# A convolution mixer's input projection computed two output blocks at a time in seven block products

## The chip, the cores and the metric

The kernel runs on one core of a Trainium2 chip. The metric is device time in microseconds of one execution; the kernel before took 1708.74 us, the median of three runs (1708.41 to 1710.8).

## The reference

Two request groups, 512 and 256 tokens, pass through a two-layer encoder trunk with model width 1024, as one row of 768 tokens. Layer 0 mixes tokens by windowed attention, layer 1 by a gated convolution of width 3. Each layer goes on with a squared-ReLU MLP of width 4096 and a gated per-layer embedding added to the residual. The change lies in the convolution mixer:

```python
def rms_norm(x, g):
    y = xf * lax.rsqrt(jnp.mean(xf * xf, axis=-1, keepdims=True) + EPS)
    return (y * g.astype(jnp.float32)).astype(x.dtype)

def short_conv(h, w_in, conv_w, w_out):
    b_gate, c_gate, u = jnp.split(h @ w_in, 3, axis=-1)
    z = c_gate * u
    zp = jnp.pad(z, ((0, 0), (half, half), (0, 0)))
    conv = zp[:, 0:s] * conv_w[0]
    for t in range(1, CONV_WIDTH):
        conv = conv + zp[:, t:t + s] * conv_w[t]
    return (b_gate * conv) @ w_out

x = x + short_conv(rms_norm(x, norm_mix[1]), conv_w_in[0], conv_w[0], conv_w_out[0])
```

`w_in` is 1024 x 3072. The convolution runs over each request group by itself.

## The kernel before

The activations lie transposed: 8 blocks of 128 channels (partitions) by 768 tokens, the residual `x(m)` in SBUF throughout. Every matrix product is computed in float32 from two-part operands: `hi` is the value rounded by ScalarE (ACT) to the matmul's `fp32r` type, `lo` is the rest, a subtraction on VectorE (DVE), and a product is `hi*hi + hi*lo + lo*hi`, three matmuls on TensorE (PE), accumulated in PSUM (`split`, `group2`). One matmul takes 128 x 128 weights and 384 tokens, half of the 768 (`H`).

The stages stand one after the other: attention, MLP 0, the gated embedding of layer 0 (`ple`), the convolution mixer (`mixer_conv`), MLP 1, the last gated embedding. Weights come from HBM in pieces of 128 x 1024 (512 KB) through three buffers (`wraw`, line 89, on SyncE's queue), and are split into `whi`/`wlo`.

In `ple`, each of 8 blocks is a gate product of 48 matmuls. Then DVE multiplies with the inverse root `rstd` (L1198), ACT takes the sigmoid (L1199), DVE multiplies with the projected embedding `pr` (L1200) and adds to `x` (L1202). `Norm.block` writes the scaled block as `hi` and `lo` (`xs_mix`, L186, L187) for the convolution, and adds its squares to an accumulator (`acc_mix`, L196). The root of the sum of squares comes later: `acc_parts` splits the accumulator (`ah`, `al`), PE sums over partitions with a matrix of ones (`ss`, L235), and DVE and ACT make `rstd` (L252 to L267). Until then products go on without it; it is multiplied into their results.

`mixer_conv` goes through 8 blocks `m`. Each takes three groups of 48 matmuls (L129): `c` with weight block 8 + m, `u` with 16 + m, `b` with m. DVE multiplies `c` with the squared `rstd` (L1281), with `u` into `z` (L1290, a row of 771 with zero columns between the groups), takes three taps of `z` (L1293 to L1295), scales `b` (L1300), multiplies both (L1301, L1302) and the result is split (`ys`, L83 and L84). Then `project_add` makes the 8 blocks of `w_out` from them, adds them to `x` (L813), and makes MLP 1's normed input.

The two MLPs already use a seven-product scheme for a product of 2 x 2 blocks of matrices (a variant of Strassen's). `Weights7` fetches two weight pieces, forms four weight sums on DVE (L392 to L398) and splits weights and sums in the groups `direct`, `second`, `s32`, `s14`, `w22`. `Norm7` keeps the normed input as four quarters (`x11`, `x12`, `x21`, `x22`) and four combinations of them (`t1` to `t4`, one `combine` per pair of blocks). `product7` (L449) is one of the seven products, 12 matmuls; PSUM banks `a`, `b`, `c`, `d` carry them, and ACT copies one bank to another (L1046, L1053, L1058) where two results share a part. The first two jobs of an MLP (`up_plain`, L978) are plain products of 96 matmuls, since combinations and `rstd` aren't there yet.

What sets the order: in the MLPs the order on PE, DVE and ACT is that of the code (`manual_schedule`); in `ple`, `mixer_conv` and `project_add` a scheduler places the instructions. SyncE's queue is always placed by it.

Of the kernel before, what the change touches and what calls it, by code (L numbers as in the profile page):

```python
# [11 lines left out]
F32 = mybir.dt.float32  # L12
F32R = mybir.dt.float32r
AF = mybir.ActivationFunctionType
ALU = mybir.AluOpType
# [32 lines left out]
def trunk_kernel(ctx: ExitStack, tc: tile.TileContext, a: dict, out: bass.AP):  # L48
# [792 lines left out]
    def first_chunk(l, norm, early):  # L841


        w = []

        def behind(i):
            if i == 4:
                w.append(up_chunk(l, 0))
# [61 lines left out]

    def mlp(l, norm, nxt, w, places, early, product=None):
# [43 lines left out]
        def up_plain(u, w, make, then):  # L955
# [11 lines left out]

            order = [(i, ks, (0, 1)) for i in range(2) for ks in ((0, 6), (6, 8))]
            if known or parts:
                order = [(i, (0, 8), (o,)) for i in range(2) for o in (1, 0)]  # L970
            for n, (i, ks, sides) in enumerate(order):
                for k in range(*ks):
                    m, h = PAIRED[k] % (KB // 2), PAIRED[k] // (KB // 2)
                    c = slice(P * m, P * m + P)
                    hi, lo = w.w[f"w{i + 1}{h + 1}"]
                    for j, (wt, part) in enumerate(((hi, 0), (hi, 1), (lo, 0))):
                        for o in sides:
                            pe.matmul(  # L978
                                ps[i][o],
                                lhsT=wt[:, c],  # L980
                                rhs=xs[f"x{h + 1}{1 + o}"][m][part],
                                start=k == 0 and j == 0,
                                stop=k == KB - 1 and j == 2,
                            )
# [45 lines left out]

        def up(u, w, make, then):


            first = u == PLAIN[l]
            w.low("s32")
            w.split("s14")
            if not first:
                late()
            v = make()
            seven = isinstance(v, Weights7)  # L1040
            a = bank("A", "a")[:, :H]
            product7(a, w, "w11", xs, True)
            if not first:
                late()
            c = bank("A" if first else "C", "c")[:, :H]
            act.activation(c, a, AF.Copy)  # L1046
            late(3 if first else 1)
            w.split("w22")
            late()
            b = bank("A" if first else "B", "b")[:, :H]  # L1050
            product7(b, w, "s3", xs, True)
            p = big("p")[:, :H]
            act.activation(p, b, AF.Copy)  # L1053
            if seven:
                v.sums32()
            product7(a, w, "s2", xs, False)
            d = bank("B", "d")[:, :H]
            act.activation(d, a, AF.Copy)  # L1058
            late(2)
            if seven:  # L1060
                v.sums14()
                v.high("s32")
            late()
            product7(c, w, "w12", xs, False)
            if seven:
                v.high("direct")
            product7(a, w, "s1", xs, False)
            y1, y2 = big("y1"), big("y2")
            dve.tensor_tensor(y2[:, H:], a, p, ALU.add)  # L1069
            rectified(y1, c, 0, H, ALU.max)  # L1070
            late()
            if seven:
                v.low("direct")
            else:
                v = [then(0)]
            product7(d, w, "w22", xs, False)
            dve.tensor_tensor(y2[:, :H], d, p, ALU.add)
            rectified(y2, y2[:], 0, T, ALU.min)
            squared(y2)
            product7(a, w, "s4", xs, False)  # L1080
            rectified(y1, a, H, T, ALU.max)
            pend.extend(acts_of(u, y1, y2, y1))
            return v
# [182 lines left out]
    def mixer_conv(norm, nxt, places, held, behind):  # L1266
        ys = [], []
        r = None
        Z = T + 3
        for m in range(KB):  # L1270
            cp = both("c")
            group2(cp, terms_of(weight(a["w_in"][KB + m], KB), norm.xs))
            up = both("u")
            group2(up, terms_of(weight(a["w_in"][2 * KB + m], KB), norm.xs))
            if r is None:
                r = norm.rstd(psum)
                r2 = slot(held[4], "rstd2", F32)
                act.activation(r2[:], r, AF.Square)
            c = big("c")
            for t, o, e in pieces(cp):  # L1280
                dve.tensor_tensor(c[:, o:e], t, r2[:, o:e], ALU.mult)  # L1281
            z = slot(held[m % 2], "z", F32, Z)
            y = slot(held[2 + m % 2], "y", F32, Z)
            s0, s1 = SEQS
            for o in (0, s0 + 1, T + 2):
                nc.gpsimd.memset(z[:, o : o + 1], 0.0)

            for o, e in ((0, H), (H, s0), (s0, T)):
                k, i = 1 + (o >= s0), o // H
                dve.tensor_tensor(z[:, o + k : e + k], c[:, o:e], up[i][:, o - i * H : e - i * H], ALU.mult)  # L1290

            n = T + 1
            dve.tensor_scalar(y[:, :n], z[:, 0:n], tap(0, m), None, ALU.mult)  # L1293
            dve.scalar_tensor_tensor(y[:, :n], z[:, 1 : 1 + n], tap(1, m), y[:, :n], ALU.mult, ALU.add)
            dve.scalar_tensor_tensor(y[:, :n], z[:, 2 : 2 + n], tap(2, m), y[:, :n], ALU.mult, ALU.add)  # L1295
            bp = both("b")
            group2(bp, terms_of(weight(a["w_in"][m], KB), norm.xs))
            b = big("b")
            for t, o, e in pieces(bp):
                dve.tensor_tensor(b[:, o:e], t, r[:, o:e], ALU.mult)  # L1300
            dve.tensor_tensor(b[:, :s0], b[:, :s0], y[:, :s0], ALU.mult)  # L1301
            dve.tensor_tensor(b[:, s0:], b[:, s0:], y[:, s0 + 1 : n], ALU.mult)  # L1302
            hi, lo = (slot(places[8 * p + m], "ys") for p in range(2))
            split(hi[:], lo[:], b[:])
            ys[0].append(hi[:])
            ys[1].append(lo[:])
        project_add(a["w_out"], ys, nxt, behind)
# [128 lines left out]
```

## Time and profile before

| | |
|---|---|
| median of the runs | 1708.74 us (1708.41 to 1710.8) |
| the profiled execution | 1711.21 us |
| its span, first to last instruction | 1709.4 us |
| mean granted TensorE clock | 0.994 |
| HBM read | 123.10 MB |

A row of the profile names the line of the kernel, the engine, the operation and its operands by the program's names, with buffer numbers left out. PEld is the loading of weights into TensorE. "Busy" is the time in which an instruction of the engine ran; matmuls overlap one another, so PE's pace is read from starts, not from lengths. In a row of a timeline the first number is the start, the second the length of the row (of several instructions, where it ends in x2 or more), and what stands in brackets is the idle time before it and what ended it. A row of the waits gives the total, the number and the longest.

### The profile page before, as it was taken

What the parts mean: (1) busy time and instruction counts of PE and PEld (TensorE: products, weight loads), DVE (VectorE), ACT (ScalarE), POOL (GpSimd) and SP (SyncE); (2) the same over time, 40 slices, a digit from 0 to 9 for tenths busy, and PEclk for the clock granted to TensorE, in tenths of its full rate; (3) what the DMA queues carried; (4) which work ended last, traced back from release to release, by engine and by line L of the source; (5) the groups of instructions that cost most, each with busy time, mean ns of one, the idle gap of its engine ahead of it and who ended that gap; (6) DMA issues with size and microseconds to landing.
All of it is one profiled execution on the core that took longest, in us unless ns stands there. A gap on an engine that the chain in (4) does not pass through costs nothing.

```text
span 1709.4 us, 24198 instructions
## 1 busy us (share of the span) xinstructions
PE 1670.7 (98%) x9542; PEld 1614.4 (94%) x9542; DVE 1346.6 (79%) x2207; ACT 858.9 (50%) x1370; POOL 2.0 (0%) x30
## 2 busy tenths in 40 slices
PE   8999999989999999999999999999999999999996
PEld 7887788989999999999999999999999999999986
DVE  6588888899999999977764444658989999999676
ACT  6367756755555445445541111445455555545454
POOL 0000000000000000000000000000000000000000
PEclk9999999999999999999999999999999999999998
DMA  8654322211222122122311111211221222212222
GB/s 259 192 138 121 115 68 81 87 54 70 74 75 73 64 74 75 66 85 88 108 62 62 62 65 67 79 50 50 74 74 64 73 75 74 70 67 87 75 89 96
DMA packets 47842, 144.59 MB, mean 85 GB/s; under 512 B 6080, under 2 KB 10688, under 8 KB 47728
## 3 DMA queue, kind: packets, MB, share of 16 engines
q1 hardware_dynamic: 45168, 139.89, 24.8%
q10 hardware_dynamic: 2560, 3.15, 0.7%
q8 instruction: 75, 1.23, 0.3%
q14 instruction: 39, 0.32, 0.1%
HBM read 123.10 MB, written 10.48 MB: 78 GB/s over the span
## 4 chain that ended last, share of the span: by engine, by line
PE 66%; DVE 23%; ACT 7%; issue 2%; DMA 0%; SPq 0%; DVEq 0%; ACTq 0%
PE a L449 14%; PE mm L129 9%; PE mm L138 8%; PE gate L129 4%; PE b L129 4%; PE c L129 4%; PE u L129 4%; PE C L449 3%; PE B L449 3%; PE b L449 3%; DVE t L344 3%; DVE wlo L428 3%; DVE y L921 3%; PE gate L138 3%; DVE zlo L428 2%
## 5 line engine op out<-in xcount | busy, mean ns | idle before, releaser
L83 ACT ACTIVATE whi<-wraw 128x1024 fp32r<-128x1024 f32 (+2 forms) x73 | 75.5, 1034 | 185.2 <-PE b L129 53.0
L417 ACT ACTIVATE whi<-sum 128x1024 fp32r<-128x1024 f32 x56 | 59.0, 1053 | 146.6 <-PE a L449 146.6
L924 ACT ACTIVATE y<-y 128x768 f32<-128x768 f32 x64 | 53.6, 838 | 139.8 <-DVE y L921 139.8
L449 PE MATMUL a<-act,whi 128*128 128x384 f32 x448 | 96.7, 337 | 0.0
L449 PE MATMUL a<-t,zhi 128*128 128x384 f32 x448 | 92.4, 338 | 3.7 <-ACT c L1046 3.7
L449 PE MATMUL b<-t,zhi 128*128 128x384 f32 x448 | 92.2, 337 | 2.6 <-ACT zhi L417 2.6
L84 DVE TENSOR_TENSOR wlo<-wraw,whi 128x1024 fp32r<-128x1024 f32 (+2 forms) x73 | 87.0, 1192 | 9.5 <-ACT whi L83 9.1
L449 PE MATMUL a<-t,whi 128*128 128x384 f32 x448 | 91.9, 337 | 0.0
L449 PE MATMUL a<-xs,whi 128*128 128x384 f32 x448 | 87.6, 337 | 0.8 <-DVE y L1069 0.8
L1102 DVE TENSOR_TENSOR x<-x,a 128x384 f32<-128x384 f32 x112 | 60.8, 553 | 33.8 <-PE a L449 33.5
L449 PEld LDWEIGHTS a<-t,zhi 128*128 128x128 f32 x448 | 79.2, 188 | 4.3 <-ACT c L1046 4.3
L138 PE MATMUL mm<-xs_mix,whi 128*128 128x512 f32 (+1 forms) x320 | 82.9, 342 | 0.0
L449 PEld LDWEIGHTS b<-t,zhi 128*128 128x128 f32 x448 | 79.4, 188 | 2.9 <-ACT zhi L417 2.9
L449 PEld LDWEIGHTS a<-xs,whi 128*128 128x128 f32 x448 | 79.0, 188 | 1.2 <-DVE y L1069 1.2
L449 PEld LDWEIGHTS a<-act,whi 128*128 128x128 f32 x448 | 79.8, 188 | 0.0
L449 PEld LDWEIGHTS a<-t,whi 128*128 128x128 f32 x448 | 79.0, 188 | 0.0
L428 DVE TENSOR_TENSOR wlo<-wraw,whi 128x1024 fp32r<-128x1024 f32 x60 | 73.2, 1220 | 5.3 <-ACT whi L417 5.3
L428 DVE TENSOR_TENSOR wlo<-sum,whi 128x1024 fp32r<-128x1024 f32 x56 | 68.4, 1222 | 9.4 <-ACT whi L417 9.4
L338 ACT ACTIVATE t<-y 128x768 fp32r<-128x768 f32 x56 | 47.1, 842 | 46.1 <-DVE y L329 35.7
L417 ACT ACTIVATE whi<-wraw 128x1024 fp32r<-128x1024 f32 x60 | 63.2, 1053 | 12.1 <-PE C L449 6.5
L428 DVE TENSOR_TENSOR zlo<-sum,zhi 128x1024 fp32r<-128x1024 f32 x56 | 68.2, 1217 | 0.0
L417 ACT ACTIVATE zhi<-sum 128x1024 fp32r<-128x1024 f32 x56 | 59.3, 1059 | 16.5 <-DVE sum L393 16.5
(290 smaller groups left out, 4629.2 us busy)
## 6 DMA issues: line engine op xcount, KB each, us to landing
wraw<-in_up SPq DMA_DIRECT2D x64, 512.0 KB, 3.5
wraw<-in_down SPq DMA_DIRECT2D x64, 512.0 KB, 3.5
wraw<-in_w_in SPq DMA_DIRECT2D x24, 512.0 KB, 3.5
wraw<-in_gate SPq DMA_DIRECT2D x16, 512.0 KB, 3.5
pj<-pjs SPq DMA_DIRECT2D x16, 384.0 KB, 3.1
wraw<-in_w_q SPq DMA_DIRECT2D x8, 512.0 KB, 5.0
wraw<-in_w_out SPq DMA_DIRECT2D x8, 512.0 KB, 3.5
x_in<-in_x SPq DMA_DIRECT2D x8, 384.0 KB, 7.0
```

Source lines behind the costliest of these rows:

```text
L83: first = act.activation(hi, src, AF.Copy)
L84: dve.tensor_tensor(lo, src, hi.bitcast(F32), ALU.subtract)
L129: pe.matmul(t, lhsT=w, rhs=x[:, o:e], start=first and i == 0 and j == 0, stop=last and i == n - 1 and j == 2)
L138: pe.matmul(ps[:, o:e], lhsT=w, rhs=x[:, o:e], start=i == 0 and j == 0, stop=i == n - 1 and j == 2,)
L338: act.activation(t[0][:], (self.q1, self.q2)[i][:], AF.Copy)
L344: dve.tensor_tensor(lo[:], (self.q1, self.q2)[i][:], hi[:].bitcast(F32), ALU.subtract)
L417: act.activation(hi[:], src, AF.Copy)
L428: dve.tensor_tensor(lo[:], src, hi[:].bitcast(F32), ALU.subtract)
L449: pe.matmul(ps, lhsT=a, rhs=b, start=start and i == 0, stop=i == len(terms) - 1, skip_group_check=True)
L921: dve.scalar_tensor_tensor(t[:, o:e], src, 0.0, r[:, o:e], op, ALU.mult)
L924: act.activation(t[:], t[:], AF.Square)
L1102: dve.tensor_tensor(t[:, o : o + H], t[:, o : o + H], f, op)
```

## The change

The projection's blocks are taken two at a time: weight blocks `m` and `m + 1` of `c`, of `u` and of `b` are one job each (`conv_chunk`), 12 jobs in all. The first two (`c` and `u` of blocks 0, 1) are plain products of 96 matmuls, the other ten take the seven products of 12. `up`'s body becomes `seven_parts`, shared by both, with the handling of results in a class (`Squares` in the MLP, `Out` here); `up_plain`'s loop becomes `plain_order` and `plain_product`. The convolution's normed input `n3` is now a `Norm7`: quarters, and combinations 0 (made during `ple`), 1, 2, 3 (made during the two plain jobs). `ple` goes through the blocks in the order 0, 4, 1, 5, 2, 6, 3, 7, and fetches and splits the first job's weights. The order on PE, DVE and ACT in `mixer_conv` is now that of the code. The first tap runs on ACT. The products `b * conv` are kept in float32 (`ys`) and split only during the last job and after it (`whole`), in places that products have freed by then.

```diff
-    def project_add(w, src, norm, behind):
+    def project_add(w, first, src, norm, behind):
         for i, m in enumerate(PAIRED):
             ps = both()
-            group2(ps, terms_of(weight(w[m], KB), src))
+            group2(ps, terms_of(weight(w[m], KB) if i else first, src))
...
+    def seven_parts(w, xs, make, then, first, late, out):
+        w.low("s32")
+        w.split("s14")
...
+        product7(a, w, "s2", xs, False)
+        d = bank("B", "d")[:, :H]
+        act.activation(d, a, AF.Copy)
+        late(2)
+        if more7:
+            v.sums14()
+            v.high("s32")
+        late()
+        product7(c, w, "w12", xs, False)
...
+        product7(a, w, "s1", xs, False)
+        out.y22(a, p)
+        out.y11(c)
...
+        product7(d, w, "w22", xs, False)
+        out.y21(d, p)
+        product7(a, w, "s4", xs, False)
+        out.y12(a)
+        return v
...
-    def ple(norm, nxt, places):
+    def ple(norm, nxt, places, behind):
         r = None
-        for m in range(KB):
+        for i, m in enumerate(PAIRED):
             gp = gate(weight(a["gate"][0, m], KB), norm.xs, 0, T)
             r = norm.rstd(psum) if r is None else r
             nxt.block(m, gated(0, m, gp, r, 0, T, nxt, places))
+            behind(i)
...
+    def conv_chunk(n):
+        m = 2 * (n // 3) + (KB, 2 * KB, 0)[n % 3]
+        return Weights7(a["w_in"][m], a["w_in"][m + 1], plain=n < 2)
...
+        def into(kind, i, src, o, e):
+            if kind == 2:
+                b = bs[i]
+                dve.tensor_tensor(b[:, o:e], src, r[:, o:e], ALU.mult)
+                return
+            for f, g, c in columns(o, e):
+                z = zs[i][:, c]
+                dve.tensor_tensor(z, (r2[:, f:g], z)[kind], src[:, f - o : g - o], ALU.mult)
...
+            def first(i):
+                act.activation(ts[i][:, :n1], zs[i][:, :n1], AF.Copy, scale=tap(0, m + i))
+            def other(t, i):
+                dve.scalar_tensor_tensor(
+                    ts[i][:, :n1], zs[i][:, t : t + n1], tap(t, m + i), ts[i][:, :n1], ALU.mult, ALU.add
+                )
...
+        def whole(m):
+            hi, lo = slot(hplaces[m], "ysh"), slot(lplaces[m], "ysl")
+            split(hi[:], lo[:], ys[m][:])
+            parts[0][m], parts[1][m] = hi[:], lo[:]
...
+                    last = n == 3 * KB // 2 - 1
+                    if last:
+                        pend.extend(lambda m=m: whole(m) for m in range(4))
+                        pend.append(lambda: (whole(4), whole(5)))
...
+                if kind == 1:
+                    pend.extend(taps())
+                elif kind == 2:
+                    pend.extend(lambda j=j, bs=bs, i=i: results(j, bs, i) for i in (1, 0))
+            late(len(pend) - 2)
+            for m in (KB - 1, KB - 2):
+                late()
+                whole(m)
+        project_add(a["w_out"], w[0], parts, nxt, behind)
...
-    n3 = Norm(1, "mix1", xs0[17:] + act0[:5], act0[5])
-    ple(n2, n3, act0[6:9])
+    n3 = Norm7(1, "mix1", xs2, x12, act0[9])
+    w2, behind = first_chunk(lambda: conv_chunk(0), n3, 1)
+    ple(n2, n3, act0[10:13], behind)
```

`late` runs the next of the pending steps (`pend`: taps, results, splits) at fixed points of a job.

Three places of the new order, each before and after. The first is DVE's row in `ple`, from the third gate's result on; `gt` is the gate, `q` and `t` are a combination's sums and their low parts, `wlo` the low part of the fifth gate's weights. Before:

```order
L1198 TENSOR_TENSOR gt<-gate,rstd_ple_8336 128x384 x2
L84 TENSOR_TENSOR wlo<-wraw,whi 128x1024
L1200 TENSOR_TENSOR gt<-pr,gt 128x768
L1202 TENSOR_TENSOR x<-x,gt 128x768
L187 SCALAR_TENSOR_TENSOR xs_mix_8487<-x,vec,xs_mix_8486 128x768
L196 TENSOR_TENSOR acc_mix_8258<-acc_mix_8258,sq 128x768
```

After:

```order
L329 TENSOR_TENSOR q<-q 128x384
L1224 TENSOR_TENSOR gt<-gate,rstd_ple_8336 128x384
L333 SCALAR_TENSOR_TENSOR q<-q 128x384
L1224 TENSOR_TENSOR gt<-gate,rstd_ple_8336 128x384
L334 SCALAR_TENSOR_TENSOR q<-q 128x384
L344 TENSOR_TENSOR t_8431<-q,t_8430 128x768
L1226 TENSOR_TENSOR gt<-pr,gt 128x768
L344 TENSOR_TENSOR t_8436<-q,t_8435 128x768
L1228 TENSOR_TENSOR x<-x,gt 128x768
L84 TENSOR_TENSOR wlo<-wraw,whi 128x1024
```

The split of the fifth gate's weights has moved behind the combination and behind the third gate's product and add.

The second is DVE's row in the projection: before, in one of the blocks `m`; after, in the first seven-part job. Before:

```order
L84 TENSOR_TENSOR wlo<-wraw,whi 128x1024
L1293 TENSOR_SCALAR y<-z,vec 128x769
L1294 SCALAR_TENSOR_TENSOR y<-z,vec,y 128x769
L1295 SCALAR_TENSOR_TENSOR y<-z,vec,y 128x769
L1300 TENSOR_TENSOR b<-b,rstd_mix_8982 128x384 x2
```

After:

```order
L428 TENSOR_TENSOR wlo<-sum,whi 128x1024
L1341 SCALAR_TENSOR_TENSOR y<-z,vec,y 128x769 x4
L428 TENSOR_TENSOR vlo<-wraw,vhi 128x512
L392 TENSOR_TENSOR sum<-wraw 128x512
L393 TENSOR_TENSOR sum<-sum,wraw 128x512
L397 TENSOR_TENSOR sum<-wraw 128x512
L398 TENSOR_TENSOR sum<-wraw,sum 128x512
L1370 TENSOR_TENSOR t<-a,p 128x384
L1330 TENSOR_TENSOR b<-c,rstd_mix_9014 128x384
```

Four taps, a half split and the next job's four sums now stand between a weight split and the add that takes PSUM bank `a`.

The third is PE's row at the start of the output projection, with the buffers' numbers: `mm_10537` and `mm_10538` are the halves of its first output block, `mm_10596` and `mm_10597` of its second; `ysh_10532` and `ysl_10533` are the parts of input block 6, the last to be split. Before, the end of the first block:

```order
L129 MATMUL mm_10402<-ys_10207,wlo_10407 128x384
L129 MATMUL mm_10403<-ys_10207,wlo_10407 128x384
L129 MATMUL mm_10402<-ys_10398,whi_10406 128x384
L129 MATMUL mm_10403<-ys_10398,whi_10406 128x384
L129 MATMUL mm_10402<-ys_10399,whi_10406 128x384
```

After:

```order
L129 MATMUL mm_10597<-ysh_10441,wlo_10601 128x384
L129 MATMUL mm_10596<-ysh_10445,whi_10600 128x384
L129 MATMUL mm_10537<-ysh_10532,whi_10491 128x384
L129 MATMUL mm_10538<-ysh_10532,whi_10491 128x384
L129 MATMUL mm_10597<-ysh_10445,whi_10600 128x384
L129 MATMUL mm_10596<-ysl_10446,whi_10600 128x384
L129 MATMUL mm_10597<-ysl_10446,whi_10600 128x384
L129 MATMUL mm_10596<-ysh_10445,wlo_10601 128x384
L129 MATMUL mm_10537<-ysl_10533,whi_10491 128x384
```

The scheduler has drawn matmuls of the second output block ahead of the first block's last two inputs.

More of the change, by code (lines that the diff above doesn't have):

```diff
@@ L965, in rects @@
                     rectified((y1, y2)[i], ps[i][o], H * o, H * o + H, ALU.max)
[L968 to L984, printed above, removed]
+            for n, (i, ks, sides) in enumerate(plain_order(known or parts)):
+                plain_product(ps, w, xs, i, ks, sides)
                 if n == 0:
@@ L1029, in up_plain @@
             return v
-        def up(u, w, make, then):
[L1034 to L1082, printed above, removed]
@@ L1083, in up @@
+        def up(u, w, make, then):
+            out = Squares()
+            v = seven_parts(w, xs, make, then, u == PLAIN[l], late, out)
+            pend.extend(acts_of(u, out.y1, out.y2, out.y1))
             return v
@@ L1264, in last_ple @@
             nc.sync.dma_start(out[m : m + n, :, s0:].rearrange("m p t -> p m t"), yb)
[L1266 to L1284, printed above, removed]
+    def conv_chunk(n):
+        m = 2 * (n // 3) + (KB, 2 * KB, 0)[n % 3]
+        return Weights7(a["w_in"][m], a["w_in"][m + 1], plain=n < 2)
@@ L1292, in mixer_conv @@
[L1292 to L1307, printed above, removed]
+        ys = {}
+        parts = [None] * KB, [None] * KB
+        def late(n=1):
+            for _ in range(n):
+                if pend:
+                    pend.pop(0)()
@@ new lines, in taps @@
+        def taps():
+            def first(i):
[3 more added lines that the diff above has]
+                    ts[i][:, :n1], zs[i][:, t : t + n1], tap(t, m + i), ts[i][:, :n1], ALU.mult, ALU.add
+                )
+            m = 2 * j
+            return [
+                lambda: (first(0), first(1)),
+                *[lambda i=i: (other(1, i), other(2, i)) for i in range(2)],
+            ]
```

167 lines of the change are left out of this document (157 added, 10 removed).

## Prediction

> **What bounds the kernel now.** I read the page's shares first, then the busy time of each engine in two stretches, then TensorE's own rows there, then who waited for whom. The page's head:
>
> ```profile
> span 1709.4 us, 24198 instructions
> PE 1670.7 (98%) x9542; PEld 1614.4 (94%) x9542; DVE 1346.6 (79%) x2207; ACT 858.9 (50%) x1370; POOL 2.0 (0%) x30
> ```
>
> TensorE (PE) is the bound, but 98% is an average over stages. The windows view gives the convolution's input projection (first row) beside a stretch of the second MLP, which already runs its products in seven parts (second row); columns are length, then PE, weight load, VectorE (DVE), ScalarE (ACT) and GpSimd busy us with their instructions, the granted clock and the DMA share:
>
> ```profile
> 870.40:1072.20 201.80, 201.80 (x1158) 201.80 (x1157) 93.94 (x134) 39.66 (x42) 0.98 (x18) 1.00 0.19 63
> 1194.78:1540.00 345.22, 344.78 (x1962) 343.15 (x1963) 314.53 (x455) 180.38 (x272) 0.00 (x0) 1.00 0.21 71
> ```
>
> In the projection PE never rests and DVE is 47% busy: fewer matmuls there are time won, and DVE has room. In the seven-part stretch DVE is 91% busy, and PE idles only 0.44 us in 345. That is the mode that the change brings into the projection. PE's pace in both, from the timeline (start, length of the merged rows, line, operands):
>
> ```profile
> 870.47 0.86 PE L129 MATMUL c<-xs_mix,whi 128*128 128x384 f32 x4
> 1072.31 0.86 PE L129 MATMUL mm<-ys,whi 128*128 128x384 f32 x4
> ...
> 1196.28 0.86 PE L449 MATMUL a<-t,zhi 128*128 128x384 f32 x4
> 1210.95 0.86 PE L449 MATMUL a<-t,zhi 128*128 128x384 f32 x4
> ```
>
> Between the first two rows lie 24 groups of 48 matmuls and the 4 of the sum of squares: 201.84 / 1156 = 0.1746 us each. Between the last two lies one job of 84: 14.67 / 84 = 0.1746. The pace is the same.
>
> **The change, part by part.**
>
> *Matmuls.* Before: 24 x 48 = 1152. After: two plain jobs of 96 and ten of 7 x 12 = 84, so 192 + 840 = 1032. 120 fewer at 0.1746 us are **-20.95 us**, all on the path. [...]
>
> *Steady load.* What DVE needs in the seven-part jobs comes from groups of the MLP stretch and of the projection before (busy us, mean ns):
>
> ```profile
> L428 DVE TENSOR_TENSOR zlo<-sum,zhi 128x1024 fp32r<-128x1024 f32 x23 | 28.0, 1217 | 0.0
> L344 DVE TENSOR_TENSOR t<-y,t 128x768 fp32r<-128x768 f32 x22 | 20.9, 952 | 0.0
> L428 DVE TENSOR_TENSOR vlo<-wraw,vhi 128x512 fp32r<-128x512 f32 x24 | 16.5, 689 | 6.8 <-ACT vhi L417 6.8
> L398 DVE TENSOR_TENSOR sum<-wraw,sum 128x512 f32<-128x512 f32 x23 | 15.8, 685 | 0.0
> L1069 DVE TENSOR_TENSOR y<-a,p 128x384 f32<-128x384 f32 x11 | 6.1, 552 | 0.0
> ```
>
> ```profile
> L1294 DVE SCALAR_TENSOR_TENSOR y<-z,vec,y 128x769 f32<-128x769 f32 x8 | 8.2, 1021 | 0.2
> L1290 DVE TENSOR_TENSOR z<-c,u 128x384 f32<-128x384 f32 x8 | 4.4, 555 | 43.3 <-PE u L129 43.3
> L1290 DVE TENSOR_TENSOR z<-c,u 128x256 f32<-128x256 f32 x8 | 3.3, 416 | 0.0
> L1290 DVE TENSOR_TENSOR z<-c,u 128x128 f32<-128x128 f32 x8 | 2.3, 282 | 0.0
> ```
>
> Weights of one job: three splits of 1.22, one of 0.69, four sums of 0.685: 7.1 us. Results: 3.2 to 3.5 us a job. Per three jobs come four taps of 1.02 and two products of 0.69 + 0.42. Together 3 x 7.1 + 10.1 + 4.1 + 2.2 = 37.7 us for 3 x 14.67 = 44.0 us of PE, 86%, less than the MLP's 91%. So in the steady state I charge **0**: PE covers it. Without that cover each microsecond over 14.67 in a job would be paid ten times.
>
> *The start.* Here the cover is thin. In the projection the sum of squares used to be consumed late; now it is taken after 48 matmuls, and the combinations, weight splits and the inverse root stand in DVE's row ahead of what PE needs. The second MLP starts in the same order of instructions, so I take its offsets. DVE's rows there, then those of the projection before, and ACT's squared scale:
>
> ```profile
> 1142.40 0.95 DVE L196 TENSOR_TENSOR acc_mlp<-acc_mlp,sq 128x768 f32<-128x768 f32 x1
> 1154.16 1.22 DVE L428 TENSOR_TENSOR zlo<-wraw,zhi 128x1024 fp32r<-128x1024 f32 x1 [1.64 <-ACT zhi L417]
> 1162.25 0.96 DVE L267 SCALAR_TENSOR_TENSOR rstd_mlp<-v,y 128x768 f32<-128x768 f32 x1
> 1163.25 1.95 DVE L921 SCALAR_TENSOR_TENSOR y<-p,rstd_mlp 128x384 f32<-128x384 f32 x4
> ```
>
> ```profile
> 876.49 0.95 DVE L196 TENSOR_TENSOR acc_mix<-acc_mix,sq 128x768 f32<-128x768 f32 x1
> 878.36 0.96 DVE L84 TENSOR_TENSOR al<-acc_mix,ah 128x768 fp32r<-128x768 f32 x1 [0.91 <-ACT ah L83]
> 893.21 0.85 ACT L1278 ACTIVATE rstd<-rstd_mix 128x768 f32<-128x768 f32 x1 [2.02 <-DVE rstd_mix L267]
> ```
>
> The last block of the gated embedding reaches its accumulator as before, at 877.44, since nothing is added in its chain. (1) PE comes to the sum of squares at 870.47 + 48 x 0.1746 = 878.85 and needs `al`, ready at 879.32, for its second matmul: 0.35. (2) The second plain job needs its `zlo`. In the MLP that ended 12.03 us after the accumulator; here that is 889.5, and PE is there at 888.6: about 1.0. (3) `rstd` ended 19.86 after the accumulator: 897.3. From there DVE does, in row: wait for the squared scale 0.9, six products into z 2.5, a split 1.22, four sums 2.74, the last combination 4 x 0.55 + 2 x 0.95 = 4.1, a split 1.22, six products 2.5, a split 1.22, four taps 4.1, the half split 0.69, four sums 2.74, and the add of `a` and `p` 0.55: 24.5 us. The twelve products and eight sums, which do not read one another, overlap like the four rows of 0.55 in 1.95, by 0.06 each, 1.2; hand-offs with ACT give back about half a microsecond. So the add ends near 921.1. Only then may PE start the job's seventh product, which it would reach unhindered at 870.47 + (192 + 4 + 72) x 0.1746 = 917.3. Whatever PE lost before counts toward this, so (1) to (3) together are **+3.8**, some 2 of it at that add. Bounds: 1.35, if DVE makes it up, and 8, if each of about ten hand-offs costs 0.5 more. Behind the late add stand the next job's splits, due at 925 and done in time by the same counting; the lag is gone after one job.
>
> PE's waits at the MLP's start, from the waits view, show the same places:
>
> ```profile
> PE a L449 <- ACT c L1046: 1.7, 1, 1.7
> PE a L449 <- DVE y L1069: 0.8, 1, 0.8
> PE b L449 <- DVE zlo L428: 0.4, 1, 0.4
> ```
>
> Their sum is 2.9. The projection has four taps more at that spot, and its accumulator comes later against PE (the gate's chain of product, sigmoid, product and add ends in it), so 3.8 is the nearer value.
>
> *The end.* Row lengths for the results' splits, in the projection before:
>
> ```profile
> L84 DVE TENSOR_TENSOR ys<-b,ys 128x768 fp32r<-128x768 f32 x7 | 6.7, 959 | 6.4 <-ACT ys L83 6.4
> L83 ACT ACTIVATE ys<-b 128x768 fp32r<-128x768 f32 x7 | 5.9, 847 | 18.2 <-DVE b L1302 18.2
> ```
>
> Count from PE's end of the last seven-part job, which begins at -14.67. DVE then does: z's last pieces to -14.0, two splits to -11.6, four taps to -7.5, the half split to -6.8, four results' splits to -3.0, the add and `c`'s product to -1.9, two more splits to 0.0, the first output weight's split to 1.2, the second add to 1.8, the second output weight's split to 3.0, the scaling to 4.0, `a`'s product to 4.5; then for each of the last two results the products 1.05, ACT's high part 0.85, the split 0.96: the high part of block 6 at 9.3, its low part at 10.3. PE's row has the second output group drawn ahead of block 6: it asks for the high part after 49 matmuls (8.6) and the low part after 55 (9.6). It is held once before, at its fifth matmul (0.7), by ACT's split of the second output weight, which needs the place of the last product's weights and so runs from 0.05 to 1.1: 0.45. So it comes to block 6 at 9.0 and waits 0.3, and 0 to 0.3 at the low part: **+1.0**. Bounds: 0, and 3.2, if the two blocks had to be waited for after 36 matmuls, in plain order.
>
> *The gated stage.* A combination and two weight splits are new in it. Of these the combination stands ahead of the split of the fifth gate's weights, which before ran here:
>
> ```profile
> 830.60 1.22 DVE L84 TENSOR_TENSOR wlo<-wraw,whi 128x1024 fp32r<-128x1024 f32 x1
> ```
>
> PE needs it four matmuls into that gate, at 870.47 - (192 - 4) x 0.1746 = 837.6. Now the combination (4.1) and the third gate's product and add (0.95 each, as the row of `acc_mix` has for this shape) come before it: 831.8 + 6.0 = 837.8, less the overlaps. **+0.2**, between 0 and 1.5. The later gates find the lag made up, since a gate's chain is shorter than its 8.4 us of PE. Moved DMAs: the first two `w_in` loads pass the last three gate loads in SP's queue; those still start as their buffers come free, a gate ahead of PE. The first `w_in` split stands in ACT's row before the first sigmoid and waits there for its load; behind it in that row are a table load and that sigmoid, whose product DVE takes up only after the second gate's, which PE brings no sooner.
>
> *Nothing:* the first tap on ACT (50% busy), 18 fewer memsets, other places. Before the gated stage and after the output projection every queue's order is unchanged.
>
> **Sum:** -20.95 + 3.8 + 1.0 + 0.2 = -15.95. The profiled execution took 1711.21 us, 2.5 above the median of the runs, 1708.74. Against it the sum gives 1695.3; against the median **1692.8 us**.
>
> **Rivals.**
>
> *No waits at all.* DVE has 14% spare and hands over in time: 1708.74 - 20.95 = 1687.8. Against it: both MLPs waited at this place. 0.10.
>
> *The clock halves.* In the first MLP two waits of PE lay close together, and the granted clock fell:
>
> ```profile
> 353.10 1.67 PE L449 MATMUL b<-t,zhi 128*128 128x384 f32 x8 [2.61 <-ACT zhi L417]
> 357.49 1.75 PE L449 MATMUL a<-t,zhi 128*128 128x384 f32 x8 [2.02 <-ACT c L1046]
> 360.32 2.48 PE L449 MATMUL c<-xs,whi 128*128 128x384 f32 x8
> ```
>
> ```profile
> 345.00:365.00 20.00, 15.37 (x78) 14.72 (x77) 18.29 (x30) 11.07 (x16) 0.00 (x0) 0.91 0.17 53
> ```
>
> 0.91 over 20 us is 3.4 us at half clock, some 1.7 us lost. The MLP that waited 2.9 in all kept its clock. My waits here (0.35, 1.0, 0.4, 2) lie 10 us and more apart, so I leave this out of the sum; with it 1694.5, twice 1696.2. 0.17. [...]
>
> *DVE becomes the bound.* Place: each job's add of `a` and `p`, which the seventh product waits for; before it in DVE's row stand the next job's four sums, and in every third job the taps. It decides once a job's row of DVE, with its own waits, is over 14.67 us. Half a microsecond over gives 1692.8 + 5 = 1697.8. For a kernel slower by over 3.4 us (1712.1) ten jobs must lose 2.0 us each: 16.7 us for 12.6 of work, 4.1 idle per job, where the MLP's DVE idles 0.09 x 14.67 = 1.3. At 2.2 each the time is 1714.8. 0.13, of it 0.04 slower and 0.02 the same.
>
> That the 120 matmuls do not go cannot be: the order of PE's instructions has them no more.
>
> **How the numbers follow.** My forecast has 0.60, 1692.8, by its own bounds 1689 to 1700. A difference under 0.2% (3.4 us) can't be told from none. The range 1688.5 to 1699.5 leaves out the lower half of the first rival (0.05) and the last one from about 0.7 a job on (0.09). Faster: 0.60 + 0.10 + 0.17 + 0.07 = 0.94; same 0.02; slower 0.04.
>
> **What would show it.** From the projection's first matmul to that of the output: 1036 x 0.1746 = 180.9 plus 3.8 us, instead of 201.84. PE's waits: on `al` (0.35), on the second job's `zlo` (1.0), on the add in the first seven-part job (2), on the second output weight and the last results (1), none in the seven-part jobs between. DVE near 86% in the seven-part jobs. It is wrong if PE waits in most jobs, if a matmul there takes over 0.18 us, or if the granted clock falls in the stretch.

## The result, and the profile after

The changed kernel took 1688.48 us, the median of four runs (1687.69 to 1690.17), beside 1708.71 for the kernel before: ratio 0.9868 with a 95% interval of 0.9855 to 0.9882. (The ratio isn't the quotient of these two medians, which is 0.9882.) The gain in medians is 20.2 us, where 15.95 was forecast. 1688.48 lies just under the range's end of 1688.5, by much less than the runs differ among themselves; that the gain was 4 us larger than forecast isn't a matter of such a margin. The profiled execution took 1687.88 us, its span 1686.0. The head of its page:

```profile
span 1686.0 us, 24120 instructions
PE 1642.6 (97%) x9422; PEld 1586.0 (94%) x9422; DVE 1408.7 (84%) x2305; ACT 907.1 (54%) x1448; POOL 1.0 (0%) x12
```

PE has 120 matmuls fewer, DVE 62 us more work. The windows view (length, then PE, weight load, DVE, ACT and GpSimd busy us, granted clock, DMA share) of the whole projection, of the same stretch of MLP 1 as before, and of three seven-part jobs in the projection, one after the other:

```profile
866.30:1049.40 183.10, 180.98 (x1037) 179.62 (x1037) 147.75 (x217) 82.90 (x110) 0.00 (x0) 1.00 0.18 64
1171.70:1517.00 345.30, 343.54 (x1961) 341.77 (x1962) 314.36 (x455) 180.53 (x272) 0.00 (x0) 1.00 0.20 71
930.70:945.28 14.58, 14.58 (x85) 14.58 (x85) 9.73 (x16) 5.07 (x7) 0.00 (x0) 1.00 0.20 74
945.28:959.86 14.58, 14.58 (x85) 14.58 (x85) 13.54 (x20) 6.74 (x9) 0.00 (x0) 1.00 0.22 72
959.86:974.44 14.58, 14.58 (x85) 14.58 (x85) 11.38 (x18) 5.06 (x7) 0.00 (x0) 1.00 0.21 73
```

In the three jobs PE doesn't rest, and DVE is busy for 34.65 us of 43.74, 79%. The forecast had 37.7 of 44.0. The clock keeps 1.00 through the stretch. PE's first matmul of the projection and of the output projection, and its waits between, with the rows around the two largest:

```profile
866.31 0.34 PE L974 MATMUL p<-xs,zhi 128*128 128x384 f32 x1
885.19 0.44 PE L974 MATMUL p<-x,zlo 128*128 128x384 f32 x1 [0.64 <-DVE zlo L428]
916.00 1.67 PE L449 MATMUL a<-xs,whi 128*128 128x384 f32 x8 [1.42 <-DVE t L1370]
930.70 1.55 PE L449 MATMUL a<-xs,whi 128*128 128x384 f32 x8
945.28 1.55 PE L449 MATMUL a<-xs,whi 128*128 128x384 f32 x8
1049.42 0.52 PE L129 MATMUL mm<-ysh,whi 128*128 128x384 f32 x2
```

The stretch took 1049.42 - 866.31 = 183.11 us instead of 201.84; 184.7 was forecast. The waits stand where they were expected, at the second job's `zlo` and at the add of `a` and `p`. But the pace, the time from one matmul's start to the next, is another: a job of 84 matmuls took 14.58, 0.17357 us each, where the kernel before took 0.17461. At the new pace 1036 matmuls are 179.8, so the start lost 3.3 us; PE idled for 2.1 of them (183.10 less 180.98), and the eight matmuls behind the wait of 1.42 took 1.67, where eight in the later jobs take 1.55.

And the projection isn't all. The two profiled executions, stage by stage, from starts of the same matmuls:

| stage | before | after | difference |
|---|---|---|---|
| start to the `rstd` transposes of the attention (L606) | 45.02 | 42.69 | -2.33 |
| MLP 0, from its second seven-part job with the up weights to its last but one | 310.71 | 309.54 | -1.17 |
| from there to the first gate product | 82.26 | 81.79 | -0.47 |
| the gates | 67.80 | 67.60 | -0.20 |
| the projection | 201.84 | 183.11 | -18.73 |
| output projection to MLP 1's first late product | 107.44 | 107.40 | -0.04 |
| from there to the last sum of squares (L235) | 519.05 | 518.51 | -0.54 |

The two stretches that the table leaves out, from the transposes to MLP 0's second such job and behind the last sum of squares, differ by less than 0.1. Without the start, the stages add up to 21.15 us. In MLP 0 the instructions of both kernels are the same, in the same order. So two questions were open: is the rest of the gain chance, or did the change make it; and is the start's loss what the forecast says it is?

### The profile page after: what moved, and what is told of

It reads as the page before. It is cut to its first block, busy times and chain, and to the rows that moved or that the text cites. A ratio compares the mean times of both kernels' runs of the same rounds, so it can differ in the third digit from the quotient of the medians.

```text
span 1686.0 us, 24120 instructions
## 1 busy us (share of the span) xinstructions
PE 1642.6 (97%) x9422; PEld 1586.0 (94%) x9422; DVE 1408.7 (84%) x2305; ACT 907.1 (54%) x1448; POOL 1.0 (0%) x12
## 5 line engine op out<-in xcount | busy, mean ns | idle before, releaser
L449 PE MATMUL a<-xs,whi 128*128 128x384 f32 x608 | 118.2, 335 | 3.2 <-DVE y L1091 1.7
L449 PE MATMUL b<-t,zhi 128*128 128x384 f32 x528 | 109.0, 339 | 3.0 <-ACT zhi L417 3.0
L449 PEld LDWEIGHTS a<-xs,whi 128*128 128x128 f32 x608 | 106.5, 188 | 4.1 <-DVE y L1091 2.4
L449 PE MATMUL a<-t,zhi 128*128 128x384 f32 x528 | 107.6, 336 | 2.4 <-ACT c L926 2.4
L449 PE MATMUL a<-t,whi 128*128 128x384 f32 x528 | 107.3, 336 | 0.0
L449 PEld LDWEIGHTS b<-t,zhi 128*128 128x128 f32 x528 | 94.3, 190 | 3.6 <-ACT zhi L417 3.6
L428 DVE TENSOR_TENSOR wlo<-wraw,whi 128x1024 fp32r<-128x1024 f32 x72 | 87.9, 1221 | 7.1 <-ACT whi L417 7.1
L449 PEld LDWEIGHTS a<-t,whi 128*128 128x128 f32 x528 | 93.2, 188 | 0.0
L83 ACT ACTIVATE whi<-wraw 128x1024 fp32r<-128x1024 f32 (+2 forms) x49 | 49.9, 1019 | 36.1 <-PE mm L129 15.0
L449 PE MATMUL b<-t,zlo 128*128 128x384 f32 x264 | 62.8, 342 | 4.4 <-DVE zlo L428 4.4
```

The costliest lines, as they stand in the source:

```text
L83: first = act.activation(hi, src, AF.Copy)
L428: dve.tensor_tensor(lo[:], src, hi[:].bitcast(F32), ALU.subtract)
L449: pe.matmul(ps, lhsT=a, rhs=b, start=start and i == 0, stop=i == len(terms) - 1, skip_group_check=True)
```

## Experiments

### Both kernels again

No edit.

> The kernel before, unchanged, against itself. Between the two profiled executions 4.0 us of the gain lie ahead of the first gate product, in work that the change does not touch (2.3 of it by 15 us, where the clock rose later in the one before). Theory A, that this is variation between executions: ratio 1 within 0.2%, and this profile's first gate product starts 1 to 4 us away from 802.67; projection 200 to 202 us, without a wait. Theory B, that an early layout of buffers in the change made it: the first gate product within 1 us of 802.67 again.

> The changed kernel, unchanged. Theory A (the gain is 120 matmuls less about 3 us of waits, the rest variation): ratio 0.988 to 0.990, the projection's stretch 183 us within 0.5 again, with PE waiting for al, the second zlo and the add of a and p, 2.3 in all. Theory B (the change also gains some 4 us elsewhere): ratio 0.986 to 0.987.

Measured: the kernel before against itself 1.0003 (0.9993 to 1.0012); the changed kernel 0.9874 (0.9858 to 0.9891), by medians 1690.11 against 1711.09, 21.0 us. The ratio lies between what the two theories of the changed kernel had. The first gate product of the kernel before started at 805.70, 3.0 later than in its first profile, so the way up to it does vary. But stages of one kernel agree to a few hundredths of a microsecond: projection 201.85 and 183.12, gates 67.79 and 67.59, the stretch of MLP 0 310.67 and 309.55. What varies is the start (up to the transposes 42.7 to 45.3 in the runs of this study, 42.74 and 42.98 in two variants of the kernel before, 44.14 and 44.9 in two of the changed one) and what the fall of the clock at MLP 0's start costs (the granted clock over 335 to 375 us was 0.91 in this run of the changed kernel and 0.96 in its first). So the first row of the table is chance, but -1.17, -0.47, -0.20 and the new pace aren't: they belong to the built program. For these stages theory A, variation between executions, falls.

### All jobs plain

```diff
-        return Weights7(a["w_in"][m], a["w_in"][m + 1], plain=n < 2)
+        return Weights7(a["w_in"][m], a["w_in"][m + 1], plain=n < 12)
...
-    ys = act0[5:13]
+    ys = xs2[20:24] + act0[9:13]
```

(`plain` is made to serve all twelve jobs, the places of the high and low parts of the results move as well.)

> All twelve jobs of the projection are plain products: 1152 matmuls as before, with all the rest of the change kept (input in quarters, combinations made though no product reads them, first tap on ScalarE, results split late; buffers of the results placed elsewhere). Theory A (the matmuls make the gain): 1688.5 + 120 x 0.1736 - 1.6 for the add's wait = 1707.7, the stretch 1156 x 0.1736 = 200.7 plus 0.8 to 1. Theory B (some 4 us come from the other edits): 1704 to 1705.

Measured: 1705.77 against 1711.09, ratio 0.9975 (0.9965 to 0.9985). With 1152 matmuls, as before, it is still faster, by 5.3 us. The projection took 202.76, 0.9 more than before, since the waits of the start are there; 96 matmuls in its later part took 16.67, 0.1736 each. The gates are 67.59, the stretch of MLP 0 309.55, and MLP 1's rest 516.88 instead of 519.05. So some 5 us come neither from fewer matmuls nor from less waiting: theory B, though not yet its cause. The 2.2 in MLP 1 are this run's own, with the results in other places; the changed kernel's rest is 518.51.

### Rows of 784, then of 832

What all these programs share against the kernel before is where their buffers lie. The four rows of `z` and `y` have 771 elements, 3084 bytes; the rest have 768, 3072. The change puts the long rows into other slots, so the slots between lie 32, 64 or 96 bytes further. The edit, in each of the two kernels, is one number:

```diff
-        Z = T + 3
+        Z = T + 16
```

> The kernel before with the four rows of z and y 784 elements wide instead of 771; no instruction differs. 771 x 4 = 3084 bytes move all places behind such a row by an odd multiple of 32 bytes, 784 x 4 by a multiple of 64, so that all moving operands of 384 columns then begin at the same place within 64 bytes as the weights do. Theory P (TensorE's pace hangs on where operands lie): the projection goes from 201.85 to 200.7 us (0.1736 a matmul, as in all_plain), the gates from 67.8 to 67.6, four jobs of MLP 0 from 59.21 to 58.96, the whole 3 to 5 us faster. Rival (the pace comes from the order of the code or the engines beside): 201.85, 67.8 and 59.21 again, ratio 1.

> The changed kernel with the same wider rows. Theory P: its projection already has the faster pace and stays at 183.1, gates 67.6; in MLP 1 four jobs go from 59.22 to 58.96, 1.6 us in all, so 0.1% faster than the changed kernel. Rival: nothing changes anywhere.

Measured: 0.9997 (0.9988 to 1.0007) and 0.987 (0.9856 to 0.9885). The projection of the kernel before went to 201.49 only, MLP 0 stayed at 310.83, the gates went to 67.38. By the addresses of the built program all but 20 of its matmuls of 384 columns now had both operands at the same place within 64 bytes, so that alone did not bring the faster pace. The gates show more. PE's rows of one of them, in the kernel before (weights begin at 160 within 256 bytes, by the addresses of the built program):

```profile
820.15 0.86 PE L129 MATMUL gate<-xs_ple,whi 128*128 128x384 f32 x4
821.19 0.85 PE L129 MATMUL gate<-xs_ple,whi 128*128 128x384 f32 x4
...
824.32 0.86 PE L129 MATMUL gate<-xs_ple,whi 128*128 128x384 f32 x4
825.37 0.87 PE L129 MATMUL gate<-xs_ple,whi 128*128 128x384 f32 x4
826.43 0.87 PE L129 MATMUL gate<-xs_ple,whi 128*128 128x384 f32 x4
```

From row to row go the six matmuls of one term. The first term, whose operands both begin at 160, takes 1.04; the last ones, whose `lo` begins at 32, take 1.05 and 1.06. Over seven gates the means are 1.043 and 1.040 for the two terms at 160, 1.047 for both with a part at 128, 1.052 to 1.054 for the four with a part at 32. In the run with 784, where the weights begin at 32, those four take 1.040. Hence the next pair, with rows of 13 x 256 bytes:

```diff
-        Z = T + 3
+        Z = T + 64
```

> The kernel before with the rows of z and y 832 elements wide (13 x 256 bytes; a normal row is 12 x 256), so that every operand of every matmul of 384 columns begins at the same place within 256 bytes; before, 1692 of 7668 had moving operand and weights at the same place. In before's gates, of whose eight terms the weights begin at 160 in 256, terms with both parts of the moving operand at 160 took 1.040 us for six matmuls, those with one part at 128 took 1.047 and with one part at 32 1.053. Theory P' (places within 256 bytes set the pace): projection 1156 x 0.1735 = 200.6, gates 67.3, four jobs of MLP 0 58.96 and of MLP 1 58.96, the whole 5 to 6 us under the kernel before, ratio 0.9965 to 0.997. Rival (widths of 784 gave what there was to have): projection 201.5, MLP 0 59.2, ratio 0.999.

> The changed kernel with rows of 832. In the changed kernel 6618 of 7548 matmuls already have both operands at the same place within 256 bytes. Theory P': projection 183.1 as it was, gates 67.3, MLP 1's four jobs 59.22 to 58.96, 2 us in all under the changed kernel: ratio to before 0.986. Rival: as the changed kernel.

Measured: 1703.31 against 1711.79, ratio 0.9951 (0.9936 to 0.9966), and 1686.6, ratio 0.9852 (0.9838 to 0.9867). The kernel before gains 8.5 us from one number, more than expected; 6.6 of them are in the stages of the table from MLP 0 on, the rest lies ahead, where executions vary. Its first matmuls of the gates, the projection and the output projection:

```profile
798.86 0.85 PE L129 MATMUL gate<-xs_ple,whi 128*128 128x384 f32 x4
866.12 0.85 PE L129 MATMUL c<-xs_mix,whi 128*128 128x384 f32 x4
1066.51 0.85 PE L129 MATMUL mm<-ys,whi 128*128 128x384 f32 x4
```

The gates take 67.26, the projection 200.39, or 0.17335 a matmul; MLP 0's stretch 309.48, MLP 1's rest 516.71. The changed kernel's gates take 67.26 as well, its projection 182.94, MLP 1's rest 516.2 (from 518.51). By the addresses of the built programs 1692 of 7668 matmuls of 384 columns had both operands at the same place within 256 bytes before, 6618 of 7548 after. With rows of 832 it is all but 20 in either kernel, and PE's pace in the projection of the kernel before is 0.7% faster (0.17461 to 0.17335); the gates, which use none of the rows that were widened, went from 67.80 to 67.26.

This pair also gives the change by itself, with all places alike: 1703.31 to 1686.6, 16.7 us. By the stages from MLP 0 on it is 17.6, of which 0.5 lie in the last row of the table. The forecast of the change's parts was 15.95.

### Four plain jobs

```diff
-        return Weights7(a["w_in"][m], a["w_in"][m + 1], plain=n < 2)
+        return Weights7(a["w_in"][m], a["w_in"][m + 1], plain=n < 4)
```

(One block has the wrong sign in this kernel, `z` of block 3, whose two factors come from jobs of different kinds; no instruction is missing.)

> Four plain jobs instead of two, eight in seven parts. Theory A (PE's count and one wait at the first seven-part job): 1688.5 + 24 x 0.1736 = +4.2, less the 1.6 of the wait for the add, which has no late combination and no squared root ahead of it any more: 1691.1, and no wait over 0.3 after the second plain job. Rival (the taps and the row of VectorE at any first seven-part job make the wait): the wait stays, 1692.7.

Measured: 1692.4, ratio 0.9889 (0.9874 to 0.9903), 2.3 over the changed kernel measured beside it (1690.11). The projection took 186.05, 2.93 more: 24 x 0.17357 = 4.17 less 1.24. The waits view of its projection has no row for the add:

```profile
PE p L974 <- DVE zlo L428: 1.1, 2, 0.6
```

The two waits are 0.64 at the second job's `zlo`, as in the changed kernel, and 0.48 at the third's, which theory A hadn't. So a seven-part job as the third one costs the wait at the add, and two jobs more of plain products cost more than they save. What of DVE's row makes that wait isn't told by this run: the taps of blocks 0 and 1 stand in plain jobs here, so the rival isn't put to the test.

### The taps, in two other places

Behind the add and the product after it:

```diff
             def y11(self, c):
                 into(self.kind, 0, c, 0, H)
+                for step in self.behind:
+                    step()
```

> In the first seven-part job alone, the taps of the first two blocks stand behind the add of a and p and the product after it, instead of ahead of them. Theory A (VectorE's row of work ahead of that add makes the 1.42 wait): the wait there goes, VectorE's later splits come no earlier, so up to 0.5 is lost at the next job's zlo: 1.1 us faster than the changed kernel. Rival (another operand is late there, the copy or the weights): the wait stays, no gain.

Measured: 1691.05, ratio 0.9888 (0.9871 to 0.9905): no gain. The waits of its projection:

```profile
PE a L449 <- DVE wlo L428: 0.9, 1, 0.9
PE b L449 <- DVE zlo L428: 0.7, 1, 0.7
PE p L974 <- DVE zlo L428: 0.7, 1, 0.7
```

The wait of 1.42 is gone and 0.87 + 0.70 have come, at the next job's low parts. In the changed kernel DVE has no gap between 893.88 and 926.8; here it waits for PE at the add,

```profile
916.17 0.56 DVE L1370 TENSOR_TENSOR t<-a,p 128x384 f32<-128x384 f32 x1 [1.27 <-PE a L449]
917.11 4.20 DVE L1341 SCALAR_TENSOR_TENSOR y<-z,vec,y 128x769 f32<-128x769 f32 x4
921.23 1.22 DVE L428 TENSOR_TENSOR wlo<-wraw,whi 128x1024 fp32r<-128x1024 f32 x1
```

and then does the taps ahead of a split that PE needs. My expectation had seen the second `zlo` and not this split. So the taps were given to the second seven-part job, in rows of 832:

```diff
-                        late,
+                        (lambda n=1: None) if n == 2 else late,
```

> after_rows_832, and the first seven-part job takes up no pending step: the four taps of blocks 0 and 1 go to the second seven-part job, behind its splits. Theory A' (VectorE's row has no gap from 893.9 to 926, so what is moved to a place where TensorE would wait for it anyway gains nothing, but the second job has about 3 us to spare): the wait of 1.42 for the first add goes and none takes its place, 1.5 us under after_rows_832. Rival (as with the taps behind the add: the lag comes out in the next job's zlo or at its add): same time as after_rows_832 within 0.4.

Measured: 1685.77, ratio 0.9848 (0.9834 to 0.9863), beside 0.9852 (0.9838 to 0.9867) without: by medians 0.8, which the intervals can't tell apart. The trace can. The projection took 181.53 instead of 182.94, and its only wait in the waits view is

```profile
PE p L974 <- DVE zlo L428: 0.6, 1, 0.6
```

1.4 us less, as theory A' has it. The row of DVE ahead of the add is what made the wait, and it can be spread over the next job.

### The weight sums made twice

```diff
         if more7:
-            v.sums32()
+            for _ in range(again):
+                v.sums32()
```

(The same for `sums14`; `again` is 2 in the projection.)

> Each seven-part job but the last makes its four weight sums twice, 2.5 to 2.7 us more of VectorE in a job. VectorE's busy time was 34.65 in three jobs, 11.55 of 14.58 each. Theory A (it has 3 us a job to spare, and only the start pays): the first add is 2.6 later, 1.42 + 2.6 = 4.0 of wait, up to 1 more in the second job, the rest free: 1688.5 + 3 = 1691.5. Theory B (the forecast's count of 12.6 a job): 15.3 a job, 0.7 over the 14.58 nine times, and the start: 1697. Theory C (it was bound already): nine times 2.6, 1712.

Measured: 1696.12, ratio 0.9918 (0.9903 to 0.9933), 6.0 over the changed kernel measured again (1690.11); the projection 189.16, 6.05 more. Three jobs in the windows view, and PE's waits at the add in the first job and at the two later ones where the taps fall:

```profile
935.00:978.70 43.70, 42.99 (x248) 42.67 (x247) 40.69 (x62) 15.59 (x22) 0.00 (x0) 1.00 0.22 73
```

```profile
920.71 2.93 PE L449 MATMUL a<-xs,whi 128*128 128x384 f32 x8 [4.07 <-DVE t L1372]
966.88 1.67 PE L449 MATMUL a<-xs,whi 128*128 128x384 f32 x8 [0.71 <-DVE t L1372]
1011.61 1.66 PE L449 MATMUL a<-xs,whi 128*128 128x384 f32 x8 [0.71 <-DVE t L1372]
```

The first wait is the 4.0 of theory A. The extra sums made DVE's work 2.0 us a job more (40.69 for 34.65 in three jobs), and it had room for nearly all of it: at 93% PE waits 0.71 in each third job, the one with the taps. What theory A had not is the clock. Behind the wait of 4.07 eight matmuls take 2.93 instead of 1.55, and the granted clock of the three microseconds from 920 is 0.58:

```profile
920.00:923.00 3.00, 2.29 (x7) 2.29 (x8) 2.97 (x6) 0.00 (x0) 0.00 (x0) 0.58 0.00 0
```

So the prediction's third rival, DVE as the bound, is right in kind, and begins near 40.69 / 3 = 13.6 us of DVE work a job, in the job that has the most.

### Results split at the end

```diff
-                    if last:
-                        pend.extend(lambda m=m: whole(m) for m in range(4))
-                        pend.append(lambda: (whole(4), whole(5)))
...
-            late(len(pend) - 2)
+            for m in range(6):
+                whole(m)
```

> The changed kernel with the first six results split after the last job instead of during it. Theory A (the splits in the last job hide 6 x 0.95 of VectorE and as much of ScalarE that the output projection would wait for): TensorE waits 4 to 5 us at its first low part, up to 1.3 more at the last blocks, and after a wait that long the clock falls for 3.4 us and costs 1.7 more: 6 to 8 us over the changed kernel. Rival (the output projection takes one block a us, as fast as the splits come): only the first wait, 4 to 5, no clock.

Measured: 1689.64, ratio 0.9874 (0.9858 to 0.989). Both expectations were far off. The output projection to MLP 1's first late product took 108.33 instead of 107.40, 0.9 more, with one wait:

```profile
1051.31 0.62 PE L129 MATMUL mm<-ysl,whi 128*128 128x384 f32 x2 [0.43 <-DVE ysl L84]
```

DVE, without the splits, idles 3.02 before the last job's add and then has the first low part done at 1051.26; from there a split each 0.95 keeps ahead of PE's 1.05 a block. I had counted DVE as late as in the changed kernel. Splitting results as places come free is worth about 1 us.

## Why the prediction was right or wrong

**The matmuls** (-20.95): right. 120 fewer, at 0.17335 with places alike 20.8 us, all of it on PE's path. With all jobs plain the projection is back at 202.76.

**The step that failed** is "Nothing: the first tap on ACT, 18 fewer memsets, other places". Other places aren't nothing: the long rows moved, and with them the pace of stages that the change doesn't touch. By the profiled executions that is 1.17 + 0.47 in and behind MLP 0, 0.20 in the gates, 1036 x 0.00104 = 1.08 in the projection and 0.44 in the output projection (as built 107.44 to 107.40, with places alike 106.90 to 107.30), 3.4 us. With 3.4 more, the forecast would have been 1689.4. Of the 5.2 us between the forecast and the 21.15 of the stages, 1.3 more come from the start, the end and the gated stage, each charged too much, and 0.5 from the last row of the table. That 0.5 isn't of this kind: with places alike it is still there (516.71 to 516.2). It lies in the last gated stage, and its cause stays open. For the pace the forecast went by two stages that agreed at 0.1746 and took it for a constant of the instruction. Two stages of one program that agree say nothing of another program, in which buffers lie elsewhere. With all places alike a matmul took 0.17335.

**The start** (+3.8): right in mechanism, 3.3 in size. Waits at `al` (875.03 is 0.21 late), at `zlo` (0.64 for 1.0) and at the add (1.42 for about 2), in the forecast's places and order. The add ended 42.8 us after the accumulator, forecast 43.7; the half microsecond that hand-offs with ACT give back in that sum was an estimate, which no row shows by itself. The taps put into the next job show that DVE's row ahead of it is the cause.

**The end** (+1.0): 0.4, by the stretch from the output projection on with all places alike (106.90 to 107.30). The waits view has no row there.

**The gated stage** (+0.2): nothing. 67.26 in both with places alike.

**The steady state** (0): right, and with more room than I counted, 79% and not 86%: DVE's instructions that don't read one another overlap by some 0.08 us (sums of 0.69 start 0.60 to 0.61 apart in the changed kernel), and I took the overlap off only at the start.

**The rivals.** No waits at all gives nearly the measured time, 1687.8, but it didn't happen: the waits are there, and the places made up for them. DVE as the bound was not reached; the doubled sums show it 2 us a job further on. The clock didn't fall in the projection (1.00).

What makes it fall the prediction had only in part. It read the waits of 2.61 and 2.02 together as the cause. In the second run of the kernel before one wait of 2.61 was enough; PE went on at 356.13 with the granted clock at 0.55:

```profile
356.13 2.93 PE L449 MATMUL b<-t,zhi 128*128 128x384 f32 x8 [2.61 <-ACT zhi L417]
```

```profile
356.00:359.60 3.60, 3.47 (x12) 3.45 (x12) 3.20 (x6) 1.38 (x3) 0.00 (x0) 0.55 0.00 0
```

Nor does the length of a wait decide it. At the same place of MLP 1, PE waited 1.82 in the run with the sums made twice, and the clock halved 1.3 us later (first two rows); it waited 1.87 in the changed kernel with rows of 784, and the clock stayed (last two):

```profile
1164.92 1.88 PE L449 MATMUL a<-t,zhi 128*128 128x384 f32 x8 [1.82 <-ACT c L926]
1166.30:1169.60 3.30, 3.30 (x12) 3.30 (x11) 3.09 (x6) 2.58 (x5) 0.00 (x0) 0.50 0.00 0
...
1158.22 1.67 PE L449 MATMUL a<-t,zhi 128*128 128x384 f32 x8 [1.87 <-ACT c L926]
1155.00:1162.00 7.00, 5.13 (x30) 4.81 (x29) 5.53 (x10) 5.35 (x9) 0.00 (x0) 1.00 0.00 0
```

In the first profiled execution of either kernel the half clock lasts 3.413 us each time but at the very end: from 212.16 and 358.93 before, from 210.92 and 350.87 after. The two beginnings lie 43 and 41 times 3.413 us apart. Cut into such stretches from 300 us to 20 us before the end, each execution has one at whose end the clock fell: PE idled 1.97 us in it before, 2.80 after, and at most 1.62 and 1.43 in any other. In the kernel before the 2.61 was divided as 1.62 and 0.99, and the fall came with the 2.02, of which 1.97 lay in one stretch. The projection's 1.42 lay in one stretch as well, and the clock stayed at 1.00. This is read off two traces; no run was made to test it, and not everything fits it. Ahead of 300 us the clock fell after 1.29 and 1.23 us of idling in a stretch, and elsewhere not after 1.67. And in the kernel before with rows of 784, behind one wait of 2.76, matmuls ran at about half pace for some 6 us from 351.88 on (eight in 2.93, four in 1.48, eight in 2.48), with a granted clock of 0.91 over 335 to 375 us.

Nothing here shows why places matter to PE: the runs show that the width of four rows does it (0.17461 to 0.17335 in the projection), and that the gates' terms whose operands begin at the same place within 256 bytes are the fast ones (1.040 and 1.043 us for six matmuls, the others 1.047 to 1.054). In these traces it was enough that the moving operands begin at another place than the weights, without a difference between the two parts. By starts and addresses, runs of eight and more matmuls whose moving operands all begin at 32 while the weights begin at 160 take 174.9 ns each in the kernel before (173.75 where all begin at 160), and those at 224 beside weights at 32 take 175.0 in the run with 784 (173.85 where all begin at 32). Whether a difference between the parts adds to it was not taken apart.

## What to carry to other kernels

The pace read from these traces was that of a placement (0.17461 and 0.17335 us a matmul in one kernel with two widths of four rows): when a change moves buffers, compare stages that it doesn't touch, and if they moved too, try rows whose length is a multiple of 256 bytes, as the 832 elements here, before explaining anything else. Isolate a change by giving both kernels the same places; here that turned 20.2 us into 16.7, near the step-by-step sum of 15.95. A wait of 1.42 us behind a full row of an engine went away here only when work went to a job with room; with the work moved by two instructions, it came back under another name.

## What was not expected of the hardware

A matmul of 384 columns in the projection took 173.35 ns with all operands beginning at the same place within 256 bytes, and 174.6 in the kernel before; one number in a row's width made that kernel 8.5 us faster (1711.79 to 1703.31). And behind a single wait of 1.82 us the granted clock was 0.50, in the run with the sums made twice, while around one of 1.87 it stayed at 1.00, in the changed kernel with rows of 784.
